# Hybrid recurrent decoder step: modulated blocks kept in two parts, S5 columns in another layout

## The chip, the cores and the metric

One core of one Trainium2 chip runs the whole step in one launch. The metric is the device time of the program in microseconds.

## What is computed

One layer on a prompt of 2048 tokens and 8 samples of 4 tokens (2080 columns), width 1024, float32 in and out. The part that the change touches:

```
mod = silu(c) @ ada_w + ada_b                     # six sections of 1024: sh1 sc1 g1 sh2 sc2 g2
h   = x * (1 + sc1) + sh1                         # modulated input
z   = h @ in_proj                                 # 1024 x 1536
gate_a, xa, xb = z[:, :512], z[:, 512:1024], z[:, 1024:]
hseq = rglru(conv4(xa, state_conv), state_h)      # RG-LRU group
y_s  = s5(xb)                                     # 32 groups of 16 columns, each a 64-wide complex diagonal state
gy   = gelu(y_s); y_b = gy * sigmoid(gy @ glu_w + glu_b)
mix  = concat(gelu(gate_a) * hseq, y_b) @ out_proj
x = layer_norm(alpha * x + g1 * mix);  then a squared-ReLU MLP with sh2, sc2, g2 and a second layer norm
```

## The kernel before

TensorE multiplies in a 4-byte format in which each operand is split into a high and a low part: a product is three matmuls (high x high, high x low, low x high). `split` makes the two parts: ScalarE copies the value into the high part, then a given engine (VectorE `V` or GpSimd `Q`) subtracts it to get the low part. The framework plans the order of the instructions of each engine ahead of time from its own estimates; an engine then works through its order and waits where data is missing. Nearly all DMAs are issued by SyncE (`SP`), in order, on one queue.

The tokens are cut into 8 blocks of 256 (block 7 has the 32 sample columns too). Two passes go over them.

First pass (to about 165 us). `make_h` loads a block of x, transposes it on TensorE, applies scale and shift into the float32 tile `hf` (two halves q of 4 x 128 features; two buffers in all), stores `hf` to the DRAM tensor `Hd` (L434), and splits it into `hh` and `hl` (the low part of half 1 on GpSimd, of half 0 on VectorE). `proj` (L373 to L375) multiplies the block by the four S5 column tiles of `in_proj`; ScalarE copies the result into `xb`, ordered by position j in a chunk of 8 tokens and chunk c, and `put_u` (L512) stores it to `Ud[m, j, p, c]`, in pieces of 32 chunks, 128 bytes. Blocks 0 and 1 (`BARE` = 2) are treated before the shift sh1 is known and get it later. Between the blocks the S5 matrices are prepared (tiles `Bx`, `CA`, `kt`).

Second pass (about 165 to 465 us). `load_w` loads and splits the eight gate and RG-LRU column tiles of `in_proj` (raw tile `rwin`, parts `hwin` and `lwin`; the low part alternates between GpSimd and VectorE). `load_h` (L553) loads a block of `Hd` again, float32, and splits it again with the low part on GpSimd (`b0l` to `b7l` in the rows). For each of 8 blocks and 8 column tiles `proj` gives one result (`accg`, 24 matmuls), stored to `Xd` or `Gd`. Sixteen S5 pairs are interleaved, one every 2.25 column tiles: `load_pair` loads `U` from `Ud` (L1743, two loads of 128 rows of 1088 bytes), matrices `M` and `Tf`, builds the rotations `E` by doubling (VectorE with ScalarE), and splits; `scan_pair` multiplies (`pv`), copies 8 columns to `VS`, scans along the chunks and splits the states (`Hh`, `Hl`); `out_pair` makes `py`. Also interleaved are the four other sections of the adaLN product: `ada_mm` adds up (`pa`), and `ada_fin` copies the sum to SBUF (`adasb`, VectorE, L190), transposes it with four small matmuls (`pm`, L193) and adds the bias. From block 5 on the RG-LRU group starts: `rg_weights` loads the conv and recurrent states `sct` and `sht` and transposes them (`pst`), `rg_conv` makes `xc` on VectorE.

Then come the GLU and output projection with the first norm (about 465 to 750 us) and the MLP; the change does not touch them.

Of the kernel before, what the change touches and what calls it, by code (L numbers as in the profile page):

```python
# [35 lines left out]
def trunk(ctx: ExitStack, tc: tile.TileContext, *args):  # L36
# [53 lines left out]
    Hd = dtile([KD, P, T], "Hd")  # L90
    Ud = dtile([4, L, P, NC2], "Ud")
# [96 lines left out]
    def ada_fin(pa, sec):  # L188
        sb = raw_tile(f"adasb{sec}")[:, 0:512]
        V.tensor_copy(sb, pa)  # L190
        pm = ptile([P, 4, 2, 9], "C", f"pm{sec}")
        for k in range(4):
            PE.matmul(pm[:, k, :], sb[:, k * P:k * P + P], sel, start=True, stop=True)  # L193
        add(V, mods[:, sec * 8:sec * 8 + 8, :].rearrange("p (n k) s -> p k n s", n=2), pm,
            vec["ada_b"][:, sec * 8:sec * 8 + 8].rearrange("p (n k) -> p k n", n=2).unsqueeze(3).to_broadcast([P, 4, 2, 9]))
# [49 lines left out]
    def rg_weights(rg):  # L245

        wgh = rg.tile([P, 2, 4, P], F32R, tag="wgh", name="wgh")
        wgl = rg.tile([P, 2, 4, P], F32R, tag="wgl", name="wgl")
        wgr = rg.tile([P, 2, 4, P], F32, tag="xc", name="wgr", bufs=2)
        Q.memset(wgr, 0.0)  # L250
        for g, key in enumerate(("rg_wr", "rg_wi")):
            src = a[key][0].rearrange("(f q) i j -> q i f j", q=2)
            for q in range(2):
                SP.dma_start(wgr[64 * q:64 * q + 64, g, :, 64 * q:64 * q + 64], src[q])
        split(wgh, wgl, wgr, Q)

        sct = rg.tile([24, 512], F32, tag="rr", name="sct")
        SP.dma_start(sct, a["state_conv"][0].rearrange("s w f -> (s w) f"))
        sht = rg.tile([8, 512], F32, tag="gi", name="sht")
        SP.dma_start(sht, a["state_rglru_h"][0])  # L260
        pst = gate_ps[0]("pst")[:, 0:128].rearrange("p (f c) -> p f c", f=4)
        for f in range(4):
            PE.transpose(pst[:, f, 0:24], sct[:, f * P:f * P + P], ident[:24, :24])
            PE.transpose(pst[:, f, 24:32], sht[:, f * P:f * P + P], ident[:8, :8])
        xas = rg.tile([P, 4, NS, 7], F32, tag="xas", name="xas")
        V.tensor_copy(xas[:, :, :, 0:3], pst[:, :, 0:24].rearrange("p f (s w) -> p f s w", w=3))
        h0s = rg.tile([P, 4, NS], F32, tag="h0s", name="h0s")
        V.tensor_copy(h0s, pst[:, :, 24:32])
        rgs.update(wgh=wgh, wgl=wgl, xas=xas, h0s=h0s, h=None)
# [92 lines left out]
    with lpool("ab") as ab:  # L362
# [31 lines left out]
        def make_h(hb):  # L394
# [10 lines left out]
            for q in range(2):  # L405
# [28 lines left out]
                SP.dma_start(Hd[4 * q:4 * q + 4, :, t0:t0 + nt].rearrange("k p t -> p k t"), hf[:, :, :nt])  # L434
                hh, hl = hs[q]
                if hb:
                    split(hh[:, :, :nt], hl[:, :, :nt], hf[:, :, :nt], Q if q else V)
                if hb == BARE:
                    split(hh[:, :, 256:258], hl[:, :, 256:258], SH1[:, 4 * q:4 * q + 4, 0:1].to_broadcast([P, 4, 2]), V)
# [68 lines left out]
        def put_u(hb, m, xb, shift=None):  # L508
            ncc = 32 + (16 if hb == 7 else 0)
            if shift is not None:  # L510
                ts(V, xb[:, :, 0:32], xb[:, :, 0:32], shift, None, ALU.add)
            u_out[hb] = SP.dma_start(Ud[m, :, :, hb * 32:hb * 32 + ncc].rearrange("j p c -> p j c"), xb[:, :, :ncc]).ins  # L512

        for hb in range(8):
# [8 lines left out]
            for m in range(4):  # L523
# [6 lines left out]
                else:  # L530
                    xb = ab.tile([P, L, 48], F32, tag="stg", name=f"xb{hb}_{m}", bufs=4)
                act(xb[:, :, 0:32], acc[:, 0:256].rearrange("p (c j) -> p j c", j=L), AF.Copy)
                if hb == 7:
                    Q.memset(xb[:, :, 40:48], 0.0)
                    Q.memset(xb[:, 0:4, 32:40], 0.0)
                    act(xb[:, 4:8, 32:40], acc[:, 256:288].rearrange("p (s j) -> p j s", j=JS), AF.Copy)
# [9 lines left out]
        def load_h(hb):  # L546
            t0, nt = piece(hb)
            hs = halves(f"b{hb}")
            for q in range(2):
                hh, hl = hs[q]  # L550
                hf = ab.tile([P, 4, 288], F32, tag="hf", name=f"hg{hb}_{q}", bufs=2)
                dst = hf[:, :, :nt]
                SP.dma_start(dst, Hd[4 * q:4 * q + 4, :, t0:t0 + nt].rearrange("k p t -> p k t"))  # L553
                if hb < BARE:
                    for kk in range(4):
                        k = 4 * q + kk
                        if kk % 2:
                            ts(V, dst[:, kk, :], dst[:, kk, :], SH1[:, k, 0:1], None, ALU.add)
                        else:
                            act(dst[:, kk, :], dst[:, kk, :], AF.Identity, bias=SH1[:, k, 0:1])  # L560
# [3 lines left out]
        wga = [load_w(m, V if m % 2 else Q, wpa if m in (4, 5, 6, 7, 0) else wpb, u_out[WB])  # L564
               for m in (4, 5, 6, 7, 0, 1, 2, 3)]
        nxt = load_h(0)
        npair = nada = 0
        spare = [f32(wslot(f"spare{i}", "l", wpb)).rearrange("p (q h c) -> p q h c", q=2, h=2) for i in range(2)]
        RG_AT = 5
        PAIR_U = [2.25 * i for i in range(17)] + [99]  # L570
        for hb in range(8):
            t0, nt = piece(hb)
            hs = nxt
            if hb < 7:
                nxt = load_h(hb + 1)
            if hb == RG_AT:
# [12 lines left out]
            for m in range(8):  # L589
# [5 lines left out]
                st = ab.tile([P, 384], F32, tag="stg", name=f"st{hb}_{m}", bufs=4)  # L595
# [3 lines left out]
                if nada < 32 and 2 * (u + 1) // 3 > nada + 1:  # L599
# [6 lines left out]
                    if k == KD - 2:  # L606
                        ada_fin(pa, sec)
# [849 lines left out]
def s5(ctx, nc, tc, a, outs, rpool, ps, ident, scratch, o):  # L1457
# [278 lines left out]
    def load_pair(p):  # L1736
# [3 lines left out]
        U = pt_([P, 2, NC2], f"U{p}", "U", bufs=2)  # L1740
        for h in range(2):
            r0 = (g0 + h) * 16
            SP.dma_start(U[:, h, :], Ud[b, :, r0:r0 + 16, :])  # L1743
# [19 lines left out]
        split(Uh, Ul, U, Q)  # L1763
# [135 lines left out]
```

## Time and profile before

| | |
|---|---|
| median of 3 runs | 2112.32 us (2111.28 to 2117.05) |
| profiled execution | 2115.44 us, its span 2113.7 us |
| granted TensorE clock, mean | 0.986 |
| TensorE busy | 2011.9 us, 95% |
| VectorE busy | 1543.5 us, 73% |
| ScalarE busy | 1087.4 us, 51% |
| GpSimd busy | 494.0 us, 23% |
| DMA queue of SyncE | 359415 packets, 485.52 MB, 69.6% of 16 engines |

A matmul's shown duration overlaps the next one, so busy TensorE is not TensorE at its peak; its waits and the spacing of its matmuls tell more. Shares over the whole span mix stages with different limits, so the stretches of the first 480 us are read one by one.

### The profile page before, as it was taken

The page shows a single profiled execution, that of the slowest core. Times are in us where ns is not written, and L with a number is a line of the kernel's source. Part 1 is how long each engine was busy: PE and PEld are TensorE (multiplying, and loading weights), DVE is VectorE, ACT ScalarE, POOL GpSimd, SP SyncE. Part 2 cuts the span into 40 slices and gives each one's busy share as a digit, 9 for nine tenths or more (in the row PEclk, how much of TensorE's full clock was granted, in tenths as well). Part 3 has the DMA queues.
Part 4 walks back from the last instruction along what each step waited for, and adds up shares of the span by engine and source line. Part 5 has one row for each costly group of instructions (what it writes and reads, how often), then busy time and mean ns, then how long its engine had stood idle before and what let it go on. Part 6 is the DMA issues. An engine that isn't in the chain of part 4 may idle for free.

```text
span 2113.7 us, 35579 instructions
## 1 busy us (share of the span) xinstructions
PE 2011.9 (95%) x13055; PEld 1904.1 (90%) x13055; DVE 1543.5 (73%) x2920; ACT 1087.4 (51%) x2077; POOL 494.0 (23%) x327
## 2 busy tenths in 40 slices
PE   7998999889999989999999899999999999999996
PEld 4897888887877879999999899999999999999996
DVE  5678897467887899989898965666747555655587
ACT  3446665445766447554646454635445344444452
POOL 2255333323433233222223300101012001010103
PEclk9999999999999999999999999999999999999998
DMA  9799765543434467968677797878678968686861
GB/s 329 177 263 274 233 197 171 141 137 80 130 94 99 134 244 265 346 248 306 239 278 264 266 323 248 305 268 288 243 260 317 315 229 282 216 270 239 265 218 54
DMA packets 363037, 489.08 MB, mean 231 GB/s; under 512 B 126939, under 2 KB 264575, under 8 KB 362863
## 3 DMA queue, kind: packets, MB, share of 16 engines
q1 hardware_dynamic: 359415, 485.52, 69.6%
q8 instruction: 103, 1.69, 0.3%
q10 hardware_dynamic: 3448, 1.29, 0.2%
q14 instruction: 71, 0.58, 0.1%
HBM read 347.73 MB, written 139.00 MB: 230 GB/s over the span
## 4 chain that ended last, share of the span: by engine, by line
PE 63%; DVE 19%; DMA 6%; issue 5%; ACT 4%; POOL 1%; SPq 1%; ACTq 0%; DVEq 0%; POOLq 0%
PE m1a L1078 19%; PE m2x L1225 13%; PE m1s L1078 8%; PE m2s L1225 6%; PE m2a L1225 3%; DVE xc L62 2%; DVE acc L44 1%; PE accg L373 1%; PE accg L374 1%; PE accg L375 1%; PE op L963 1%; PE pa L185 1%; PE op L964 1%; PE op L962 1%; DVE gi L347 1%
## 5 line engine op out<-in xcount | busy, mean ns | idle before, releaser
L44 POOL TENSOR_TENSOR y<-y,ln_g 128x512 f32<-128x512 f32 (+3 forms) x28 | 36.5, 1320 | 645.8 <-ACT y L65 544.2
L65 ACT ACTIVATE hid<-hid 128x346 f32<-128x346 f32 (+1 forms) x240 | 116.1, 489 | 71.1 <-DVE hid L62 64.3
L65 ACT ACTIVATE ht<-hid 128x692 fp32r<-128x692 f32 (+1 forms) x92 | 72.0, 783 | 127.8 <-PE m2a L1225 38.9
L44 DVE TENSOR_TENSOR lt<-hid,ht 128x692 fp32r<-128x692 f32 (+1 forms) x92 | 85.2, 927 | 40.5 <-ACT ht L65 40.5
L44 DVE TENSOR_TENSOR acc<-m2x,acc 128x346 f32<-128x346 f32 (+1 forms) x168 | 84.1, 511 | 32.0 <-PE m2x L1225 31.7
L44 DVE TENSOR_TENSOR hid<-hid,hid 128x692 f32<-128x692 f32 (+1 forms) x92 | 87.1, 947 | 23.5 <-ACT hid L65 23.3
L1225 PE MATMUL m2x<-ht,hw2s 128*128 128x348 f32 (+1 forms) x352 | 87.7, 322 | 1.8 <-DVE acc L44 1.8
L62 DVE SCALAR_TENSOR_TENSOR hid<-m1s,vecB,u 128x346 f32<-128x346 f32 (+1 forms) x94 | 53.5, 573 | 45.0 <-ACT u L65 35.4
L65 ACT ACTIVATE u<-m1a 128x346 f32<-128x346 f32 (+1 forms) x96 | 43.5, 453 | 70.4 <-PE m1a L1078 63.0
L44 DVE TENSOR_TENSOR lb<-hid,hb 128x692 fp32r<-128x692 f32 (+1 forms) x69 | 69.2, 1004 | 4.7 <-ACT hb L65 4.5
L65 ACT ACTIVATE hb<-hid 128x692 fp32r<-128x692 f32 (+1 forms) x69 | 53.8, 783 | 21.6 <-PE m2a L1225 6.9
L1225 PEld LDWEIGHTS m2x<-ht,hw2s 128*128 128x128 f32 x352 | 61.9, 189 | 2.2 <-ACT hw2s L65 2.1
L65 ACT ACT_TABLE_LOAD x40 | 51.3, 1283 | 15.9 <-DVE hgb L57 6.5
L44 DVE TENSOR_TENSOR acc<-m2s,acc 128x346 f32<-128x346 f32 (+1 forms) x120 | 55.7, 508 | 4.1 <-PE m2s L1225 4.0
L1078 PE MATMUL m1s<-h2t13h,hw1s 128*128 128x348 f32 (+1 forms) x200 | 54.1, 329 | 3.9 <-DVE x L62 3.5
L1225 PE MATMUL m2x<-lt,hw2s 128*128 128x348 f32 (+1 forms) x176 | 56.1, 321 | 0.9 <-DVE lt L44 0.9
L1225 PE MATMUL m2x<-ht,w2s 128*128 128x346 f32 (+1 forms) x216 | 55.9, 321 | 0.0
L1225 PE MATMUL m2s<-ht,hw2s 128*128 128x348 f32 (+1 forms) x208 | 53.2, 331 | 2.6 <-ACT ht L65 2.6
L44 DVE TENSOR_TENSOR u<-m1s,u 128x346 f32<-128x346 f32 (+1 forms) x48 | 24.7, 514 | 42.0 <-PE m1s L1078 27.2
L65 ACT ACTIVATE y<-y,AB,mods 128x128 f32<-128x128 f32 (+2 forms) x96 | 37.5, 472 | 34.5 <-DMA y<-Cd 34.5
L1225 PE MATMUL m2a<-hb,hw2a 128*128 128x348 f32 (+1 forms) x200 | 52.0, 327 | 3.4 <-DVE acc L44 3.4
L1078 PE MATMUL m1a<-h2b1h,hw1a 128*128 128x348 f32 (+1 forms) x208 | 55.1, 323 | 0.0
(854 smaller groups left out, 7982.0 us busy)
## 6 DMA issues: line engine op xcount, KB each, us to landing
W1d<-hw1s SPq DMA_DIRECT2D x53, 512.0 KB
W2d<-hw2s SPq DMA_DIRECT2D x53, 512.0 KB
w1s<-W1d SPq DMA_DIRECT2D x45, 512.0 KB
lw1s<-W1d SPq DMA_DIRECT2D x43, 512.0 KB
hw2s<-W2d SPq DMA_DIRECT2D x41, 512.0 KB
hw1s<-W1d SPq DMA_DIRECT2D x40, 512.0 KB
w2s<-W2d SPq DMA_DIRECT2D x40, 512.0 KB
lw2s<-W2d SPq DMA_DIRECT2D x39, 512.0 KB
```

The lines of the kernel that those rows point to most:

```text
L44: return eng.tensor_tensor(out=out, in0=in0, in1=in1, op=op)
L62: return V.scalar_tensor_tensor(out, in0, s, in1, op0, op1)
L65: return S.activation(out, in_, f, **kw).ins
L185: PE.matmul(pa[q:q + 32, :], cT[:, k + e, :], w[:, n * 512:n * 512 + 512], start=(k == 0), stop=(k == KD - 2), tile_position=(0, q))
L347: V.tensor_tensor_scan(gi[:, f, :n], rr[:, f, :n], gi[:, f, :n], 0.0 if pi == 0 else rgs["h"][:, f:f + 1], ALU.mult, ALU.add)
L373: PE.matmul(acc[:, :nt], wh[:, k, :], hh[:, kk, :nt], start=(k == 0), stop=False)
L374: PE.matmul(acc[:, :nt], wh[:, k, :], hl[:, kk, :nt], start=False, stop=False)
L375: PE.matmul(acc[:, :nt], wl[:, k, :], hh[:, kk, :nt], start=False, stop=(k == KD - 1))
L962: PE.matmul(ac[:w, :], yh[:, kk, o:o + w], wh[:, hs], start=(k == 0), stop=False)
L963: PE.matmul(ac[:w, :], yl[:, kk, o:o + w], wh[:, hs], start=False, stop=False)
L1078: PE.matmul(ps, x[:, k, :], h[:, k, o:o + w], start=(on is None and k + i == 0), stop=(k == 3 and i == 2), skip_group_check=on is not None)
L1225: PE.matmul(ps[2 * s_ + jj], x[:, f, js], h[:, f, :], start=(fresh and n + f + e == 0), stop=(n == len(pairs) - 1 and f + e == 3), skip_gr ...
```

## The change

Five edits. Blocks 2 to 7 of the modulated input are no longer stored as float32 `Hd` but as their two parts in a new tensor `Hsd`, after the split; the second pass loads the parts straight into `hh` and `hl` and splits nothing for these blocks. `Ud` gets the layout [tile, column, block, position, chunk], so that a block's columns are stored as rows of 1 KB (2 KB for block 7, whose sample columns become a ninth block), and the load of a pair gathers its [position x column] rows from pieces of 32 chunks. The low parts of all gate weights are made on VectorE. `ada_fin` is cut in two: the copy to SBUF comes where it was, the small matmuls three column tiles later. The conv and recurrent states are loaded at block 4 into the `hf` buffers, not inside `rg_weights`.

```diff
-    Hd = dtile([KD, P, T], "Hd")
-    Ud = dtile([4, L, P, NC2], "Ud")
+    Hd = dtile([KD, P, 512], "Hd")
+    Hsd = dtile([2, KD, P, T], "Hsd")
+
+    Ud = dtile([4, P, 9, L, 32], "Ud")
...
-    def ada_fin(pa, sec):
+    def ada_out(pa, sec):
         sb = raw_tile(f"adasb{sec}")[:, 0:512]
         V.tensor_copy(sb, pa)
+        return sb
+
+    def ada_fin(pa, sec, sb=None):
+        if sb is None:
+            sb = ada_out(pa, sec)
...
-        sct = rg.tile([24, 512], F32, tag="rr", name="sct")
-        SP.dma_start(sct, a["state_conv"][0].rearrange("s w f -> (s w) f"))
-        sht = rg.tile([8, 512], F32, tag="gi", name="sht")
-        SP.dma_start(sht, a["state_rglru_h"][0])
+        sct, sht = rgs["in"]
...
-                SP.dma_start(Hd[4 * q:4 * q + 4, :, t0:t0 + nt].rearrange("k p t -> p k t"), hf[:, :, :nt])
+                if hb < BARE:
+                    SP.dma_start(Hd[4 * q:4 * q + 4, :, t0:t0 + nt].rearrange("k p t -> p k t"), hf[:, :, :nt])
                 hh, hl = hs[q]
                 if hb:
                     split(hh[:, :, :nt], hl[:, :, :nt], hf[:, :, :nt], Q if q else V)
+                if hb >= BARE:
+                    for i, x in enumerate((hh, hl)):
+                        SP.dma_start(Hsd[i, 4 * q:4 * q + 4, :, t0:t0 + nt].rearrange("k p t -> p k t"), f32(x[:, :, :nt]))
...
-            u_out[hb] = SP.dma_start(Ud[m, :, :, hb * 32:hb * 32 + ncc].rearrange("j p c -> p j c"), xb[:, :, :ncc]).ins
+            n = 2 if hb == 7 else 1
+            u_out[hb] = SP.dma_start(Ud[m, :, hb:hb + n].rearrange("p b j c -> p (b j c)"), xb.rearrange("p j c -> p (j c)")).ins
...
                 hh, hl = hs[q]
+                if hb >= BARE:
+                    for i, x in enumerate((hh, hl)):
+                        SP.dma_start(f32(x[:, :, :nt]), Hsd[i, 4 * q:4 * q + 4, :, t0:t0 + nt].rearrange("k p t -> p k t"))
+                    continue
...
-        wga = [load_w(m, V if m % 2 else Q, wpa if m in (4, 5, 6, 7, 0) else wpb, u_out[WB])
+        wga = [load_w(m, V, wpa if m in (4, 5, 6, 7, 0) else wpb, u_out[WB])
...
+            if hb == RG_AT - 1:
+                rgs["in"] = [ab.tile([P, 4, 288], F32, tag="hf", name=f"rgin{i}", bufs=2).rearrange("p f t -> p (f t)")
+                             [:n, 0:512] for i, n in enumerate((24, 8))]
+                SP.dma_start(rgs["in"][0], a["state_conv"][0].rearrange("s w f -> (s w) f"))
+                SP.dma_start(rgs["in"][1], a["state_rglru_h"][0])
...
                     if k == KD - 2:
-                        ada_fin(pa, sec)
+                        fins.append((u + 3, pa, sec, ada_out(pa, sec)))
+                while fins and u >= fins[0][0]:
+                    ada_fin(*fins.pop(0)[1:])
...
-        U = pt_([P, 2, NC2], f"U{p}", "U", bufs=2)
+        U = pt_([P, 2, 288], f"U{p}", "U", bufs=2)
         for h in range(2):
             r0 = (g0 + h) * 16
-            SP.dma_start(U[:, h, :], Ud[b, :, r0:r0 + 16, :])
+            SP.dma_start(U[:, h, :].rearrange("p (b c) -> p b c", c=32), Ud[b, r0:r0 + 16].rearrange("k b j c -> j k b c"))
...
-        split(Uh, Ul, U, Q)
+        split(Uh, Ul, U[:, :, 0:NC2], Q)
```

## Rows read from the trace of the kernel before

**Rows 1.** Stretches: limits, length, busy us and instructions, clock, DMA share, GB/s.

```profile
75.00:165.00 90.00, 85.70 (x737) 82.85 (x737) 68.27 (x99) 43.93 (x90) 40.27 (x29) 0.98 0.99 253
165.00:205.00 40.00, 36.17 (x279) 32.49 (x278) 35.93 (x53) 24.43 (x51) 24.51 (x14) 0.96 0.94 262
205.00:400.00 195.00, 186.05 (x1464) 158.02 (x1462) 156.09 (x357) 114.43 (x311) 61.80 (x57) 1.00 0.67 200
409.00:419.00 10.00, 9.60 (x80) 9.39 (x80) 0.46 (x1) 8.08 (x15) 6.99 (x3) 1.00 0.40 138
```

(The five busy columns are PE, PEld, DVE, ACT and POOL.)

**Rows 2.** TensorE in order of time: start, us, work, idle before and its releaser.

```profile
161.72 0.40 PE L373 MATMUL accb<-a7h,hwin 128*128 128x288 f32 x1 [1.63 <-ACT xb L65]
184.31 0.60 PE L1780 MATMUL pv<-Uh,Mh 128*128 128x272 f32 x1 [3.12 <-DVE VS L1785]
250.80 0.39 PE L1780 MATMUL pv<-Uh,Mh 128*128 128x272 f32 x1 [0.89 <-ACT Mh L65]
290.26 0.39 PE L1827 MATMUL py<-Hh,Mh 64*128 64x272 f32 x2 [2.24 <-ACT Hh L65]
334.35 0.39 PE L1827 MATMUL py<-Hh,Mh 64*128 64x272 f32 x2 [1.46 <-ACT Hh L65]
378.10 0.21 PE L263 MATMUL pst<-ident,sct 24*128 24x24 f32 x1 [1.00 <-DMA sct<-in_state_conv_dram]
403.84 1.47 PE L193 MATMUL pm<-sel,adasb 128*128 128x18 f32 x6 [4.97 <-DVE adasb L190]
```

**Rows 3.** Stretches as in rows 1, at the lower clock.

```profile
183.70:187.20 3.50, 2.89 (x13) 2.89 (x14) 1.89 (x6) 2.30 (x5) 0.00 (x0) 0.51 0.96 323
402.20:409.10 6.90, 5.26 (x25) 5.26 (x25) 2.30 (x8) 1.34 (x3) 0.00 (x0) 0.51 0.78 145
```

**Rows 4.** VectorE in order of time around 400 us.

```profile
383.71 4.95 DVE L62 SCALAR_TENSOR_TENSOR xc<-xa,vecB,xc 128x256 f32<-128x256 f32 x12
...
396.00 7.19 DVE L62 SCALAR_TENSOR_TENSOR xc<-xa,vecB,xc 128x256 f32<-128x256 f32 x12
403.11 0.68 DVE L190 COPY adasb<-pa 128x512 f32<-128x512 f32 x1
```

**Rows 5.** In order of time: a split's copy and subtraction, and VectorE's scans.

```profile
192.15 1.26 DVE L1795 TENSOR_TENSOR_SCAN V<-rho,V 128x256 f32<-128x256 f32 x2
194.73 1.06 ACT L65 ACTIVATE b2h<-hg 128x1024 fp32r<-128x1024 f32 x1 [0.99 <-PE accg L375]
...
280.13 3.40 DVE L1795 TENSOR_TENSOR_SCAN V<-rho,V 128x256 f32<-128x256 f32 x2
280.19 5.51 POOL L44 TENSOR_TENSOR b4l<-hg,b4h 128x1024 fp32r<-128x1024 f32 x2 [3.21 <-ACT b4h L65]
```

**Rows 6.** DMA packets of 92 to 95.5, 398.9 to 400, 404.9 to 406.2 us.

```profile
DMA packets 4022, 0.51 MB, mean 145 GB/s; under 512 B 4022, under 2 KB 4022, under 8 KB 4022
...
DMA packets 1027, 0.13 MB, mean 118 GB/s; under 512 B 1027, under 2 KB 1027, under 8 KB 1027
q1 hardware_dynamic: 1027, 0.13, 75.0%
...
DMA packets 409, 0.42 MB, mean 322 GB/s; under 512 B 0, under 2 KB 409, under 8 KB 409
```

(The first are stores of S5 columns, the second one load of `Yd` in 128-byte pieces, the third a load in 1-KB rows.)

**Rows 7.** Issues of the pair's load and of the block's store: shortest, median, longest ns.

```profile
L1743 SPq DMA_DIRECT2D U<-Ud x32: 577/617/1910, 163.1 to 323.2; - x32
L434 SPq DMA_DIRECT2D Hd<-hf x16: 359/686/2795, 20.0 to 147.9; - x16
```

**Rows 8.** In order of time at the seam: GpSimd and VectorE.

```profile
176.80 2.38 POOL L44 TENSOR_TENSOR lwin<-rwin,hwin 128x1024 fp32r<-128x1024 f32 x1
181.09 2.34 POOL L44 TENSOR_TENSOR b1l<-hg,b1h 128x1024 fp32r<-128x1024 f32 x1 [1.90 <-ACT b1h L65]
...
181.38 2.46 DVE L62 SCALAR_TENSOR_TENSOR E<-E,et 128x128 f32<-128x128 f32 x2 [0.79 <-ACT et L65]
185.94 1.23 DVE L44 TENSOR_TENSOR lwin<-rwin,hwin 128x1024 fp32r<-128x1024 f32 x1 [1.61 <-ACT hwin L65]
```

More of the change, by code (lines that the diff above doesn't have):

```diff
@@ L508, in put_u @@
         def put_u(hb, m, xb, shift=None):
-            ncc = 32 + (16 if hb == 7 else 0)
             if shift is not None:
-                ts(V, xb[:, :, 0:32], xb[:, :, 0:32], shift, None, ALU.add)
-            u_out[hb] = SP.dma_start(Ud[m, :, :, hb * 32:hb * 32 + ncc].rearrange("j p c -> p j c"), xb[:, :, :ncc]).ins
+                ts(V, xb, xb, shift, None, ALU.add)
+            n = 2 if hb == 7 else 1
+            u_out[hb] = SP.dma_start(Ud[m, :, hb:hb + n].rearrange("p b j c -> p (b j c)"), xb.rearrange("p j c -> p (j c)")).ins
         for hb in range(8):
@@ L530, in trunk @@
                 else:
-                    xb = ab.tile([P, L, 48], F32, tag="stg", name=f"xb{hb}_{m}", bufs=4)
-                act(xb[:, :, 0:32], acc[:, 0:256].rearrange("p (c j) -> p j c", j=L), AF.Copy)
+                    xb = ab.tile([P, 16, 32], F32, tag="stg", name=f"xb{hb}_{m}", bufs=4)[:, 0:16 if hb == 7 else L]
+                act(xb[:, 0:L], acc[:, 0:256].rearrange("p (c j) -> p j c", j=L), AF.Copy)
                 if hb == 7:
-                    Q.memset(xb[:, :, 40:48], 0.0)
-                    Q.memset(xb[:, 0:4, 32:40], 0.0)
-                    act(xb[:, 4:8, 32:40], acc[:, 256:288].rearrange("p (s j) -> p j s", j=JS), AF.Copy)
+                    Q.memset(xb[:, L:16], 0.0)
+                    act(xb[:, 12:16, 0:8], acc[:, 256:288].rearrange("p (s j) -> p j s", j=JS), AF.Copy)
                 if hb >= BARE:
@@ L553, in load_h @@
                 SP.dma_start(dst, Hd[4 * q:4 * q + 4, :, t0:t0 + nt].rearrange("k p t -> p k t"))
[L554 to L560, printed above, removed]
+                for kk in range(4):
+                    k = 4 * q + kk
+                    if kk % 2:
+                        ts(V, dst[:, kk, :], dst[:, kk, :], SH1[:, k, 0:1], None, ALU.add)
+                    else:
+                        act(dst[:, kk, :], dst[:, kk, :], AF.Identity, bias=SH1[:, k, 0:1])
                 split(hh[:, :, :nt], hl[:, :, :nt], dst, Q)
             return hs
-        wga = [load_w(m, V if m % 2 else Q, wpa if m in (4, 5, 6, 7, 0) else wpb, u_out[WB])
+        wga = [load_w(m, V, wpa if m in (4, 5, 6, 7, 0) else wpb, u_out[WB])
                for m in (4, 5, 6, 7, 0, 1, 2, 3)]
@@ L567, in trunk @@
         npair = nada = 0
+        fins = []
         spare = [f32(wslot(f"spare{i}", "l", wpb)).rearrange("p (q h c) -> p q h c", q=2, h=2) for i in range(2)]
@@ L594, in trunk @@
                 acc = proj(wga[m], hs, nt, f"accg{hb}_{m}")
-                st = ab.tile([P, 384], F32, tag="stg", name=f"st{hb}_{m}", bufs=4)
+                st = ab.tile([P, 512], F32, tag="stg", name=f"st{hb}_{m}", bufs=4)
                 act(st[:, :nt], acc[:, :nt], AF.Copy if m < 4 or hb in RAW_GATE else AF.Gelu_apprx_tanh)
```

## The prediction

> **What bounds the kernel now.** I read the table of stretches first, to see which engine is close to its limit where, then TensorE's waits in order of time in the two projection passes, then what the engine that ended each wait had been doing, and last the DMA packets around. Everything that the change touches lies before 480 us; behind that the code is the same, so whatever is won or lost before 480 us is taken to reach the end unchanged.
>
> In the table of stretches [rows 1] TensorE is busy 85.7 of 90 us in the first pass (75 to 165 us), 36.2 of 40 at the seam between the passes and 186 of 195 in the second pass. Undisturbed it issues 80 matmuls in 10 us, 0.12 us each. So TensorE bounds these passes, and only its waits can be won. VectorE is nearly full as well (35.9 of 40 at the seam, 156 of 195 in the second pass), and the DMA engines are full until 205 us (0.99, 0.94) and at 0.67 after.
>
> The waits are few [rows 2]; in brackets stands what ended each. 1.63 us at 161.72 (a staged S5 column tile not yet free); 3.12 us at 184.31 (VectorE's copy of VS); 0.89, 2.24 and 1.46 us at 250.80, 290.26 and 334.35 (pairs, behind ScalarE copies that follow VectorE); 1.00 us at 378.10 (the load of the conv state); 4.97 us at 403.84 (VectorE's copy of the last adaLN sum). [...] TensorE works again from 184.31 and 403.84, so it loses half of 2.9 and of 5.3 us: 1.45 and 2.6 us.
>
> **Part 1, the adaLN sum finished later.** At 403.11 VectorE gets to the copy that section 5's sum waits for, after twelve convolution steps that took 7.19 us; twelve like them took 4.95 us before [rows 4]. The change issues the copy as before and its TensorE half three column blocks later. A block is 24 matmuls, 2.9 us, so 8.6 us of other matmuls stand between, more than the wait of 4.97. They need only their blocks, loaded long before. What is late next is nothing that I see: the same VectorE steps also lose the GpSimd work of part 2. Gain 4.97 + 2.6 = 7.6 us. If the planner leaves the sum where it is, the wait shrinks only by the 2.2 us that the steps were held up.
>
> **Part 2, the blocks stored as two parts.** For blocks 2 to 7 the second pass loses its split: twelve ScalarE copies of about 1.06 us and twelve GpSimd subtractions of about 2.4 us (two of them, 5.51 us, at 280.19) [rows 5]. TensorE waits for none of them. They count through VectorE: two scans that take 1.26 us at 192.15 take 3.40 us at 280.13, exactly while GpSimd subtracts block 4's lower part [rows 5], and the pair behind them is the wait of 2.24 us at 290.26. The waits at 250.80 and 334.35 follow blocks 3 and 5 in the same way. These three are 4.6 us; I take 4.0, since GpSimd keeps the pairs' own subtractions, which VectorE meets too.
>
> It costs DMA. Each block moves 1.05 MB more out and 1.05 MB more in (block 7 1.18). Rows of 1 KB move at 322 GB/s [rows 6], 3.1 us for 1 MB. Blocks 3 to 7, 5.4 MB, go out in the first pass from 75 us on: +16.7 us; block 2 goes out in the idle time before. In, block 2 costs 3.3 us at the seam and blocks 3 to 7 16.7 us later. On SP's queue it is twelve more issues out and twelve more in, at about 0.6 us as other issues there [rows 7]. A store now waits for GpSimd's or VectorE's lower part instead of the sum alone, and S5 column stores and x loads queue behind it. In return the hf buffers wait for no store any more, so block 0 of the second pass can be loaded earlier.
>
> **Part 3, the S5 columns.** Stores of 128-byte pieces run at 145 GB/s: 4022 pieces in 3.5 us, 0.87 us for a store of 1024 [rows 6]. In rows of 1 KB it is 0.41 us, so 29 stores of the first pass give back 13 us. The pair's load now takes 1152 pieces of 128 bytes. The nearest row is the load of Yd, 1024 such pieces in 75% of 1.1 us, 0.83 us [rows 6], so 0.93 us against 0.43 us for 139 KB in long rows: +0.5 us for each of 32 loads. Its issue on SP takes 0.62 us now [rows 7]; a source of four indices has no row, and I keep 0.6 to 1.2 us.
>
> Added up, the DMA engines have 89 + 16.7 - 13 = 93 us of work in the 90 us of the first pass; at the seam 37.6 + 3.3 + 8 x 0.5 = 45 in 40; after it 131 + 16.7 + 12 = 160 in 195. They come up to 8 us late by 205 us and catch up afterwards. x and adaLN loads are issued 10 us or more ahead, gate weights are not. The cost lies between 0 and 8 us; I take 2. The wait at 161.72 could go (faster column stores) or grow (two parts of block 7 ahead of them); I take 0.
>
> [...]
>
> **Part 4, the gate weights' lower parts on VectorE.** Four subtractions leave GpSimd (2.38 us each) and cost VectorE 1.23 us each [rows 8], 4.9 us in a stretch where it is 90% busy. Against that, two rotation steps on VectorE take 2.46 us at 181.38 while GpSimd works on block 1 from 181.09 [rows 8]; work of that kind is what stands ahead of the VS copy that TensorE waits for at 184.31. Block 1 is still split on GpSimd, only earlier. The wait with its clock loss is 3.12 + 1.45 = 4.6 us; I take half, 2.3. The added VectorE work costs 0 to 2 us of it where GpSimd would not have blocked it; I take 0.5.
>
> **Part 5, the states loaded a block earlier.** The wait of 1.00 us at 378.10 goes. Two loads leave SP's queue in front of the convolution; they are hidden under block 4.
>
> **Sum.** -7.6 - 4.0 - 2.3 - 1.0 + 2 + 0.5 = -12.4 us. The profiled execution took 2115.44 us, which gives 2103; the median of the runs shown is 2112.32, and against it the forecast is **2100 us**.
>
> **Rivals.** (a) All named waits close and DMA costs nothing: 7.6 + 4.6 + 4.6 + 1.0 + 1.6 = 19.4 us, 2093, and some us less if freed VectorE also shortens waits too small to stand in the rows. For it: VectorE is nearly full. Against: the DMA sums. (b) DMA takes it back: the full 8 us late on TensorE's path, the 184.31 wait stays, and the edits give 7.6 + 1.0 + 4.0 - 8 - 2 = 2.6 us: 2110; or the sum of part 1 stays where it was: 2107. (c) Slower: the turning load. After 205 us the DMA engines have 195 - 131 - 16.7 = 47 us free for 24 loads, so the load may cost up to 0.43 + 2 = 2.4 us before the engines, and TensorE waiting for U, are the bound of the second pass. At 3.3 us per load it is 24 x 0.9 = 22 us over: 2100 + 22 = 2122. For it: no row shows this pattern, and SP's in-order queue would feel a split into several issues as well. Against: the Yd load at 0.83 us. [...]
>
> **How the numbers follow.** Forecast 0.50 (2093 to 2106); (a) 0.14 (2086 to 2093); (b) 0.21 (2106 to 2118); (c) 0.13; (d) 0.02. About 0.3%, 6.3 us, is what a measurement of this kernel can tell from no change: faster is under 2106. So faster 0.64, same 0.21, slower 0.15. The range goes from 2088, half of (a), to 2117, nearly all of (b); what is left out is 0.07 below and 0.16 above.
>
> **What would show it.** Right: no TensorE wait for adasb near 400 us and no low clock there; no scan at twice its length in the second pass; DMA share under 0.9 after 205 us; a U load that takes about 1 us. Wrong: TensorE waits that a DMA ends (U, rwin, ada) between 150 and 210 us, S5 column tiles not free, VectorE waiting at the seam, or another order of the planner with new waits that no row of before shows.

## The result, and the profile after

| | before | after |
|---|---|---|
| median | 2113.15 us (6 runs, 2109.27 to 2117.05) | 2136.03 us (6 runs, 2129.22 to 2143.06) |
| ratio after / before | | 1.0112, 95% interval 1.0087 to 1.0136 |
| profiled execution, its span | 2115.44, 2113.7 us | 2129.22, 2127.4 us |
| first pass ends | 164.9 us | 161.8 us |
| second pass ends | 463.6 us | 479.4 us |
| second pass to the end | 1650.1 us | 1648.0 us |

The change makes the kernel 1.1% slower. The ends of the passes are the starts of the last matmuls on `accb` and `accg`. The profiled execution after is the fastest of its six, so that the passes add up to 13.7 us of the 22.9 us between the medians. The first pass gained 3.1 us; the second takes 317.6 us for 298.7; behind it nothing moved. Block 4 of the second pass begins at 348.6 us for 322.4, so from 3 us ahead the kernel fell 26 behind, 29 us lost while the S5 pairs run. Blocks 6 and 7, where the adaLN wait was, won 8 back (68.9 us before, 394.7 to 463.6; 61.0 after, 418.4 to 479.4).

The table of stretches of the kernel after (limits, length, busy us of PE, PEld, DVE, ACT, POOL, clock, DMA share, GB/s), to be held against [rows 1]:

```profile
75.00:165.00 90.00, 88.13 (x762) 86.00 (x760) 66.66 (x95) 44.10 (x88) 34.80 (x23) 0.98 0.99 329
165.00:205.00 40.00, 36.39 (x275) 33.39 (x273) 30.94 (x65) 24.37 (x58) 11.93 (x10) 0.91 0.76 195
205.00:400.00 195.00, 170.69 (x1270) 141.93 (x1269) 131.27 (x326) 92.83 (x279) 28.15 (x43) 0.96 0.79 218
400.00:480.00 80.00, 74.86 (x595) 71.87 (x594) 44.09 (x75) 42.99 (x74) 28.50 (x13) 1.00 0.55 158
```

From 205 to 400 us TensorE is busy 171 us for 186 before, at a clock of 0.96 for 1.00. VectorE is no longer full (131 for 156 us); as the kernel is 26 us behind there, this alone does not show that part 2 freed it. On the mean the DMA engines are not full (0.79). What TensorE waited for from 205 to 350 us, after and then before (line, releaser: us in total, times, longest):

```profile
PE py L1838 <- ACT Th L65: 9.6, 4, 4.7
PE pa L187 <- DMA ada<-in_ada_w_dram: 6.4, 2, 5.4
PE pv L1798 <- ACT Mh L65: 4.6, 4, 1.9
PE pa L187 <- DMA hada<-in_ada_w_dram: 2.2, 2, 2.0
```

```profile
PE py L1827 <- ACT Hh L65: 3.7, 2, 2.2
PE pv L1780 <- ACT Mh L65: 1.4, 2, 0.9
PE pv L1782 <- DVE Ml L44: 1.0, 3, 0.6
PE py L1827 <- DVE Hl L44: 0.4, 1, 0.4
```

After, these are 22.8 us of waits for data that a load brings (`Th` and `Mh` are the copies of the loaded `Tf` and `M`); before, the list has 6.5 us, of which 2.4 for the parts of `M` and none for `Th` or a load. The waits for the scanned states (`Hh`, `Hl`), 4.1 us before, are gone. One of the waits for `Th`, followed back in order of time on SP's queue, ScalarE and TensorE, with the stretch behind it:

```profile
267.72 1.28 SPq L1851 DMA_DIRECT2D Yd<-Yt  x2
...
269.64 0.38 SPq L1764 DMA_DIRECT2D M<-BCd  x1
...
273.82 0.61 SPq L1761 DMA_DIRECT2D U<-Ud  x1
274.53 4.98 SPq L1851 DMA_DIRECT2D Yd<-Yt  x2
279.56 0.60 SPq L1761 DMA_DIRECT2D U<-Ud  x1
280.26 2.43 SPq L1764 DMA_DIRECT2D M<-BCd  x1
282.74 1.28 SPq L1766 DMA_DIRECT2D M<-BCd  x2
284.12 1.01 SPq L614 DMA_DIRECT2D Xd<-st  x2
285.22 0.40 SPq L1770 DMA_DIRECT2D Tf<-Td  x1
288.29 0.42 ACT L65 ACTIVATE Th<-Tf 128x256 fp32r<-128x256 f32 x1 [5.04 <-DMA Tf<-Td]
288.76 0.59 PE L1838 MATMUL py<-Uh,Th 128*128 128x272 f32 x1 [4.71 <-ACT Th L65]
287.00:290.00 3.00, 1.24 (x5) 1.24 (x6) 1.05 (x4) 1.67 (x6) 0.00 (x0) 0.50 0.92 243
```

The column behind the start is how long SP was at an issue. The two stores of `Yd` behind the turned `U` load hold SP for 4.98 us, the `M` load behind the second one for 2.43; the same issues took 1.28 and 0.38 us at 267.72 and 269.64, so these two alone put `Tf` 5.8 us late. ScalarE waits 5.04 us for it, TensorE 4.71, and the clock falls to 0.50. And while SP is held, the packets of three stretches:

```profile
DMA packets 301, 0.95 MB, mean 318 GB/s; under 512 B 48, under 2 KB 75, under 8 KB 301
q1 hardware_dynamic: 301, 0.95, 97.1%
DMA packets 627, 0.18 MB, mean 178 GB/s; under 512 B 606, under 2 KB 606, under 8 KB 625
q1 hardware_dynamic: 625, 0.15, 67.8%
DMA packets 510, 0.08 MB, mean 77 GB/s; under 512 B 504, under 2 KB 509, under 8 KB 509
q1 hardware_dynamic: 509, 0.07, 47.0%
```

These are 274.5 to 277.5, 277.5 to 278.5 and 278.5 to 279.5 us. In the first 3 us the engines are busy (97%) with 0.95 MB, for the most part the 4-KB rows of the two adaLN loads that SP issued at 272.83 and 273.32, ahead of the `U` load. Only then come 1110 pieces under 512 bytes, nearly all of the 1152 of the load issued at 273.82. They take some 2.0 us, with the engines at 68% and 47%; SP is let go as they end, at 279.5. So the pieces of the turned load stand about 3 us behind that traffic and then take 2 us to move, and SP waits for both.

### The profile page after: what moved, and what is told of

It is laid out like the page before. It is cut to its first block, busy times and chain, and to the rows that moved or that the text cites. A ratio compares the mean times of both kernels' runs of the same rounds, so it can differ in the third digit from the quotient of the medians.

```text
span 2127.4 us, 35544 instructions
## 1 busy us (share of the span) xinstructions
PE 2019.1 (95%) x13055; PEld 1910.7 (90%) x13055; DVE 1526.2 (72%) x2924; ACT 1076.6 (51%) x2065; POOL 456.0 (21%) x307
## 4 chain that ended last, share of the span: by engine, by line
PE 63%; DVE 19%; DMA 7%; issue 4%; ACT 4%; SPq 2%; POOL 1%; ACTq 0%; DVEq 0%; POOLq 0%
PE m1a L1096 19%; PE m2x L1243 13%; PE m1s L1096 8%; PE m2s L1243 6%; PE m2a L1243 3%; DVE xc L62 1%; DVE acc L44 1%; PE pa L187 1%; PE accb L378 1%; PE accb L377 1%; PE accb L379 1%; PE accg L377 1%; PE accg L378 1%; PE accg L379 1%; DVE gi L351 1%
## 5 line engine op out<-in xcount | busy, mean ns | idle before, releaser
L980 PE MATMUL op<-hwo,ybh 128*128 128x512 f32 x128 | 51.6, 406 | 2.8 <-ACT ybh L65 2.8
L65 ACT ACTIVATE hid<-m1a,vecB 128x346 f32<-128x346 f32 (+1 forms) x48 | 26.2, 547 | 53.7 <-PE m1a L1096 53.6
```

Of the source, the lines that this page charges most:

```text
L65: return S.activation(out, in_, f, **kw).ins
L980: PE.matmul(ac[:w, :], yh[:, kk, o:o + w], wh[:, hs], start=(k == 0), stop=False)
```

## The experiments

The theory, called T1 in the expectations, was that the pair's turned load is the loss, by holding SP's in-order queue; the rivals (T2, T3) were the doubled transfers of the two-part blocks, the gate parts on VectorE, and another order of the planner, which plans all engines anew whenever a transfer's shape changes. In the table, passes and end are those of the profiled execution in us, the ratio is that to the kernel before in runs on the same chip.

| kernel | median | ratio (95%) | first pass ends | second pass takes | second pass to end |
|---|---|---|---|---|---|
| without part 3 | 2119.11 | 1.0032 (1.0019 to 1.0044) | 174.0 | 291.4 | 1656.1 |
| without part 2 | 2136.20 | 1.0120 (1.0090 to 1.0149) | 171.3 | 306.8 | 1653.5 |
| part 3 alone | 2143.04 | 1.0139 (1.0113 to 1.0165) | 173.6 | 307.8 | 1665.3 |
| long rows, planned anew | 2105.68 | 0.9968 (0.9947 to 0.9990) | 161.7 | 279.3 | 1657.6 |
| long rows, order of after | 2102.97 | 0.9953 (0.9938 to 0.9968) | 164.1 | 285.2 | 1653.4 |
| turned, order of long rows | 2139.09 | 1.0124 (1.0105 to 1.0142) | 161.7 | 315.2 | 1659.6 |
| 512 pieces | 2114.59 | 1.0001 (0.9991 to 1.0012) | 161.1 | 295.3 | 1657.4 |
| 1152 pieces, other walk | 2115.97 | 1.0022 (1.0011 to 1.0032) | 161.6 | 297.3 | 1655.2 |
| U on ScalarE's queue | 2138.43 | 1.0121 (1.0098 to 1.0145) | 161.8 | 313.8 | 1662.7 |
| Tf on ScalarE's queue | 2127.35 | 1.0065 (1.0049 to 1.0082) | 161.1 | 310.1 | 1654.7 |
| part 1 alone | 2114.49 | 1.0005 (0.9996 to 1.0014) | 163.9 | 294.7 | 1651.4 |
| part 2 alone | 2118.92 | 1.0025 (1.0016 to 1.0034) | no comparable trace | | |
| parts 1, 4, 5 | 2114.70 | 1.0005 (0.9996 to 1.0014) | 165.2 | 299.2 | 1647.1 |
| part 1, split off ScalarE | 2126.58 | 1.0065 (1.0050 to 1.0080) | 163.8 | 295.7 | 1665.2 |
| paired stores | 2101.65 | 0.9948 (0.9931 to 0.9965) | 159.2 | 283.8 | 1655.4 |
| paired stores, no part 2 | 2119.68 | 1.0032 (1.0020 to 1.0043) | 166.6 | 295.8 | 1655.7 |

### Which part

**Without part 3.** Layout, store and load of `Ud` as before, the rest as after.

```diff
-    Ud = dtile([4, P, 9, L, 32], "Ud")
+    Ud = dtile([4, L, P, NC2], "Ud")
...
+            SP.dma_start(U[:, h, :], Ud[b, :, r0:r0 + 16, :])
```

> The changed kernel with part 3 alone undone (S5 columns stored and loaded as before; the other four parts stay). Theory T1, that the pair's turning load (1152 pieces of 128 bytes) is the loss, by holding SP's in-order queue: the 25 to 28 us lost between 194 and 349 us go, the adaLN sum's 7.9 us stay won, some us of the first pass may be given back since column stores of 1024 pieces return; 2098 to 2107 us, ratio 0.993 to 0.998 to the kernel before. Rival T2, that the doubled transfers of the two-part blocks are the loss: the second pass stays long, 2125 us or more. Rival T3, that VectorE's added gate parts or another order of the planner is the loss: 2125 us or more too.

The loss in the second pass went (291.4 us, 7.3 less than before), so there is none without part 3. But it was slower than the theory's 2098 to 2107: the first pass ends 9.1 us late. Its DMA share from 75 to 165 us is 1.01, and TensorE does 674 matmuls there for 762 in the kernel after:

```profile
75.00:165.00 90.00, 80.17 (x674) 76.94 (x672) 55.74 (x87) 36.99 (x67) 30.31 (x14) 0.97 1.01 273
```

**Without part 2.** `Hd` for all blocks and the split on load again.

```diff
-                if hb >= BARE:
-                    for i, x in enumerate((hh, hl)):
-                        SP.dma_start(Hsd[i, 4 * q:4 * q + 4, :, t0:t0 + nt].rearrange("k p t -> p k t"), f32(x[:, :, :nt]))
```

> The changed kernel with part 2 alone undone (blocks stored once as before and split again on load). T1 (the turning load): still slower than before, 2125 to 2140 us, and SP's issues of U loads still up to 4 us and more. T2 (the two-part blocks): 2100 to 2110 us.

In time as the theory said: without the two-part blocks the kernel is as slow. But its second pass takes 306.8 us for the 317.6 of the kernel after, 8.1 above the kernel before; the other 10 us of its loss (profiled executions) lie in the first pass (171.3 for 164.9) and behind the second. So the turned load costs without part 2 too, and more beside it, as far as two programs that were planned apart can show.

**Part 3 alone**, in the kernel before (the diff of the change's `Ud`, `xb`, `put_u` and `U` lines).

> The kernel before with part 3 alone. T1: it carries the whole loss without the 8 us of the adaLN sum, 2128 to 2142 us, with TensorE waits between 205 and 350 us that ScalarE's Th or the adaLN loads end. T2 and T3: 2100 to 2113 us, since the column stores of the first pass get faster.

In time slightly above the theory's range, but not by its account alone. Of the 33 us in the profiled executions 9.1 lie in the second pass (307.8 us), 8.7 in the first (173.6 for 164.9) and 15.2 behind the second. Here, and in the run without part 2, the first pass itself ends 6 to 9 us late, at a DMA share of 0.77 to 0.80, with TensorE waiting 4.3 and 5.5 us for `xb` copies from 110 to 180 us. These programs were planned anew throughout; which reordering does it was not settled. That the time met the theory is in part luck.

### The load, or the plan

**Long rows.** The 147 KB of a load in 128 rows of 1152 bytes; the S5 input then lies in another order, so the output is not the layer's, but the amount of work is the same (this holds for the next runs with exchanged patterns too).

```diff
-            SP.dma_start(U[:, h, :].rearrange("p (b c) -> p b c", c=32), Ud[b, r0:r0 + 16].rearrange("k b j c -> j k b c"))
+            SP.dma_start(U[:, h, :], Ud[b, r0:r0 + 16].rearrange("k b j c -> k (b j c)").rearrange("k (j x) -> j k x", j=L))
```

> The changed kernel, but each pair's load reads the same 147 KB in rows of 1152 bytes, so 128 pieces for 1152; the S5 input is then in the wrong order, the work is the same. T1: as with the old layout or a little better, 2095 to 2107 us, U issues on SP back at about 0.6 us. If something else in the new layout (the larger U tile, the padded last block, the stores) costs the time: 2125 us or more.

At the upper end of what was expected, 30 us below the kernel after. But the planner's order is another one too, which the next two runs take apart: the planned program is kept, with every order and wait, and only the access patterns of the 32 loads are exchanged behind the planner.

```diff
         trunk(tc, *args)
+    reread(nc, False)
...
+                    sa, da = [[288, 8], [2304, 16], [1, 288]], [[576, 128], [1, 1], [1, 288]]
+                rows[i] = x.__replace__(ins=[s.__replace__(ap=sa, bass_ap=None)], outs=[d.__replace__(ap=da, bass_ap=None)])
```

> The planned program of the changed kernel, instruction for instruction in its order and with its waits, but with the 32 U loads re-pointed after planning to rows of 1152 bytes (the S5 input is then in the wrong order). The earlier run with long rows was also planned anew, so its 30 us could be the load itself or the other order. If the load itself is the cost: about as that run, 2100 to 2110 us. If the plan made for the turned load is the cost: 2125 us or more. Half and half lies between.

The other way round the long rows are planned and the turned pattern `[[32, 8], [256, 144], [1, 32]]` is put in:

> The reverse: the order planned for the long rows, with the U loads turned after planning (the output is that of the changed kernel). If the load itself is the cost: 2125 to 2140 us, with SP's issues of U loads up to 4 us and more again. If the plan is the cost: about 2106 us.

The load itself it is: 33 us in one order (2136.03 to 2102.97), 33 us in the other (2139.09 to 2105.68); the order counts for 3. Issue and waits of the same program with long rows, from 205 to 350 us (the `U` issue's shortest, median and longest in ns, then TensorE's waits), and the `U` issue of the kernel after:

```profile
L1780 SPq DMA_DIRECT2D U<-Ud x32: 594/620/1871, 168.4 to 315.9; - x32
PE pv L1817 <- ACT Mh L84: 1.0, 2, 0.6
PE pa L206 <- DMA ada<-in_ada_w_dram: 0.3, 1, 0.3
```

```profile
L1761 SPq DMA_DIRECT2D U<-Ud x32: 597/616/5837, 165.2 to 346.9; - x32
```

The median issue is the same; the longest is 5.84 us for 1.87. TensorE's waits fall from 22.8 to 1.3 us. With the clock of 0.96 for 1.00 over 195 us, at most 7.8 us, this is up to 29 of the 32.4 us between the two second passes.

A long-row load is not done much sooner. One is issued at 266.38 us, and its pieces move until about 269.7; in the last of these microseconds little else moves, 101 pieces at a DMA share of 0.32. But SP is not held behind it:

```profile
266.38 0.62 SPq L1780 DMA_DIRECT2D U<-Ud  x1
268.89 1.31 SPq L1870 DMA_DIRECT2D Yd<-Yt  x2
DMA packets 101, 0.11 MB, mean 112 GB/s; under 512 B 9, under 2 KB 99, under 8 KB 101
q1 hardware_dynamic: 101, 0.11, 31.8%
```

The two `Yd` stores behind it are issued in 1.31 us, the first of them while it moves (the packets are 268.5 to 269.5 us). So by these two stretches (4.98 us behind 1152 pieces, 1.31 us behind 128) what holds SP is the number of pieces in the queue, more than the time of the transfer; the next section varies that number.

### What makes the load slow

**512 pieces** of 288 bytes, same plan, same bytes (`sa, da = [[72, 8], [576, 64], [1, 72]], [[576, 128], [72, 4], [1, 72]]`).

> The planned program of the changed kernel with the U loads re-pointed to the same bytes in 512 pieces of 288 bytes instead of 1152 of 128 (the S5 input is then in the wrong order). 128 pieces gave 2103 us, 1152 gave 2136. If the cost goes by the number of pieces: 33 x 384 / 1024 = 12 us above 2103, 2112 to 2118 us. If there is a threshold that 512 pieces stay under: 2103 to 2107 us.

12 us above long rows (10 by the ratios), as the count of pieces says; 512 pieces are not free.

**1152 pieces, other walk:** same pieces and addresses, but `[[256, 144], [32, 8], [1, 32]]`, so that the 144 pairs of column and block are the outermost index and the 8 positions the inner one.

> The planned program of the changed kernel, its U loads still 1152 pieces of 128 bytes from the same addresses, but walked with the 144 (column, block) pairs outermost and the 8 positions inside (the S5 input is then in the wrong order). If half of the DMA engines is what makes the load slow: a load's pieces arrive in about 1.0 us instead of 2.0, the DMA share in such a stretch is 0.9 and not 0.5, and the kernel takes 2105 to 2118 us. If the number of pieces alone counts, whatever the engines: 2130 us or more.

The same pieces cost 13 us above long rows (15 by the ratios) instead of 33. From 211 to 212 us, and from 308 to 309, where such loads run, and last a microsecond of the kernel after, 227.5 to 228.5, in which only a turned load moves:

```profile
DMA packets 1478, 0.24 MB, mean 239 GB/s; under 512 B 1427, under 2 KB 1477, under 8 KB 1477
q1 hardware_dynamic: 1477, 0.23, 131.1%
...
DMA packets 1662, 0.22 MB, mean 216 GB/s; under 512 B 1655, under 2 KB 1662, under 8 KB 1662
q1 hardware_dynamic: 1662, 0.22, 135.9%
...
DMA packets 793, 0.10 MB, mean 101 GB/s; under 512 B 793, under 2 KB 793, under 8 KB 793
q1 hardware_dynamic: 793, 0.10, 64.3%
```

In that microsecond the turned load moves 793 pieces at a share of 0.64, the other walk up to 1655 at 1.36. Worked out from these shares of 16 engines, a piece takes the same engine time in both, 13 ns, so no single piece is slower in the turned load; half as many are under way at once (the pieces and the shares both differ by a factor of 2.1). Why they are half was not shown: whether the turned load goes over half of the engines, as the expectation supposes, can't be read here, since the trace has the engines' share together and not by number.

So the number of pieces alone is not the price (the other walk has as many and costs 13 us for 33), and the outermost index alone is not either: the long rows have 8 there like the turned load, and the kernel is 33 us faster with them.

### The queue

**U on ScalarE's queue.**

```diff
-            SP.dma_start(U[:, h, :].rearrange("p (b c) -> p b c", c=32), Ud[b, r0:r0 + 16].rearrange("k b j c -> j k b c"))
+            S.dma_start(U[:, h, :].rearrange("p (b c) -> p b c", c=32), Ud[b, r0:r0 + 16].rearrange("k b j c -> j k b c"))
```

> The changed kernel with the U loads issued on ScalarE's queue, still turned. If the turned load costs by holding SP's queue: SP's other issues are short again (below 1 us for Tf and M) and the waits for Tf go, while ScalarE is held instead at its own issues; ScalarE is busy half of the time there, so 2105 to 2125 us. If the DMA engines are too slow with 128-byte pieces: Tf, M and U stay late, 2130 us or more.

Half right: SP is free, `Tf` issues take 0.58 us at most. But the hold moved with the load, and nothing was won. The issue rows and TensorE's longest wait from 165 to 350 us:

```profile
L1761 ACTq DMA_DIRECT2D U<-Ud x32: 589/1144/7447, 162.6 to 344.1; - x32
L1770 SPq DMA_DIRECT2D Tf<-Td x16: 359/384/576, 169.1 to 358.4; - x16
PE accg L377 <- ACT st L65: 18.4, 5, 7.6
```

ScalarE is held up to 7.4 us in an issue, and the copies out of PSUM stand behind it.

**Tf on ScalarE's queue**, `U` on SP:

```diff
-        SP.dma_start(Tf, bass.AP(tensor=td.tensor, offset=td.offset, ap=[[512, P], [16 * 512, 8], [1, 32]]))
+        S.dma_start(Tf, bass.AP(tensor=td.tensor, offset=td.offset, ap=[[512, P], [16 * 512, 8], [1, 32]]))
```

> The changed kernel with only the 16 loads of Tf, the largest wait behind SP's queue (35.7 us of ScalarE's waits), issued on ScalarE's queue. If SP's queue is what makes them late: the wait of Th for Tf goes and with it the TensorE waits for Th (10.5 us), 2115 to 2127 us. If the DMA engines make them late: no change, 2130 us or more.

9 us better than the kernel after, just outside what a held SP queue was to give: ScalarE's waits for `Tf` fall from 35.7 to 9.3 us (165 to 500 us), and TensorE's waits for `Th` go. Waiting behind SP is a real part of the price. The other 24 us of the 33 are not recovered by this; `M` and the adaLN weights still stand behind SP, and TensorE waits 2.7 and 4.3 us for them from 205 to 350 us.

### The other parts

**Part 1 alone** (`ada_out`, `fins`), in the kernel before.

> The kernel before with part 1 alone (the adaLN sum's small matmuls three column tiles later). By the prediction -7.6 us, 2105 us, with no TensorE wait for the copy adasb and no low clock near 405 us. If the wait only moves: 2110 us or more.

No gain, though the second pass ends 5.0 us earlier: what follows, up to the last GLU matmul, takes it back (463.6 to 703.6 us before, 458.6 to 703.4 here). Blocks 6 and 7 gain 8 us as in the kernel after (397.8 to 458.6); the blocks ahead of them, planned anew, lose 4. **Parts 1, 4 and 5:**

> The kernel before with parts 1, 4 and 5 and neither of the two layout edits. By the prediction's terms -7.6 - 2.3 + 0.5 - 1.0 = -10.4 us: 2102 us. If the two-part blocks of part 2 are needed for that (VectorE freed of GpSimd's subtractions): 2105 us or more. A rival, that other plans move the later stages by as much: anywhere from 2098 to 2112.

No gain either, and here not even at the end of the second pass. In order of time:

```profile
412.00 1.06 ACT L65 ACTIVATE hgy<-gy 128x1024 fp32r<-128x1024 f32 x1 [7.88 <-DMA gy<-Yd]
412.97 0.37 ACT L65 ACTIVATE st<-accg 128x256 f32<-128x256 f32 x1
413.39 0.58 PE L375 MATMUL accg<-b6h,hwin 128*128 128x256 f32 x1 [4.59 <-ACT st L65]
```

The wait for the adaLN copy, 4.97 us [rows 2], is gone; in its place ScalarE waits 7.88 us for the load of `gy` (the first GLU block), and the copy `st` that frees TensorE's bank stands behind it: 4.59 us.

**Part 1 with that split taken off ScalarE:**

```diff
+            Q.tensor_copy(gyh[:, :, :n], gy[:, :, :n])
+            sub(Q, gyl[:, :, :n], gy[:, :, :n], f32(gyh[:, :, :n]))
```

> Part 1 alone, with the first GLU block's split taken off ScalarE (both steps on GpSimd), so that ScalarE's copies out of PSUM no longer stand behind the load of gy. If that wait is where part 1's 7.6 us went: the second pass ends 6 to 10 us before that of the kernel before, and 2104 to 2109 us. If the next stage takes it back in any case: 2112 us or more, with the second pass still early.

Wrong: the second pass ends where part 1 alone ended, and the stages behind lose 14 us (1665.2 for 1651.4), TensorE waiting 11.7 us for VectorE in the GLU (5.8 in part 1 alone). The run tested little: in part 1 alone ScalarE waits only 1.90 us for `gy`, the 7.88 us belong to parts 1, 4 and 5 together. Whether the split on GpSimd or the new plan costs the 14 us was not settled.

**Part 2 alone:**

> The kernel before with part 2 alone (blocks 2 to 7 stored as two parts, S5 columns still stored in 1024 pieces). The DMA engines then have 89 + 16.7 = 106 us of work in the 90 us of the first pass: if that counts, the first pass ends 8 to 12 us late, and against the 4 us that VectorE gains the kernel is slower, 2116 to 2122 us. If the transfers are hidden: 2108 us.

Slower by 5 us, as full DMA engines in the first pass would have it; that the first pass is the place was not shown in this run.

### A version that beats both

**Paired stores.** Old layout and long-row load; the columns of two blocks wait in one tile and are stored in 256-byte pieces. The other four parts stay; the loads of x and of the gate weights are let go by the stores of other blocks, since there are fewer stores.

```diff
-                    xb = ab.tile([P, L, 48], F32, tag="stg", name=f"xb{hb}_{m}", bufs=4)
+                    if hb % 2 == 0:
+                        xpair[m] = ab.tile([P, L, 80 if hb == 6 else 64], F32, tag="stg2", name=f"xb{hb}_{m}", bufs=6)
+                    xb = xpair[m]
+                at = 32 * (hb % 2) if hb >= BARE else 0
...
-                if hb >= BARE:
+                if hb >= BARE and hb % 2:
                     put_u(hb, m, xb)
```

> Parts 1, 2, 4 and 5 with the old layout of the S5 columns, loaded in long rows, but the columns of blocks 2 and 3, 4 and 5, 6 and 7 stored together, in pieces of 256 bytes instead of 128: half the pieces. With single stores this was 2119 us, its first pass ending 9 us late. If the store pieces were that loss: the first pass ends at 161 to 166 us and the kernel takes 2103 to 2110 us, below both kernels. If the two-part stores were it: 2115 us or more.

2101.65 us, 0.5% below the kernel before and 1.6% below the kernel after. **The same without part 2:**

> The same paired stores with parts 1, 4 and 5, without the two-part blocks. Single stores gave 2114.7 us. The first pass has DMA time to spare here without them, so its end moves by 3 us at most: 2108 to 2115 us. If this is as fast as the run with part 2, part 2 is worth nothing by itself.

Slower than expected and than the kernel before. Between the two, part 2 is worth 18 us, 12 of them in the second pass (295.8 to 283.8) and 7 in the first (166.6 to 159.2); as the two were planned apart, how much of this is the plan is open. VectorE's 32 scans, with part 2 and without, as groups (busy us, mean ns):

```profile
L1820 DVE TENSOR_TENSOR_SCAN V<-rho,V 128x256 f32<-128x256 f32 x32 | 20.8, 674 | 0.0
```

```profile
L1811 DVE TENSOR_TENSOR_SCAN V<-rho,V 128x256 f32<-128x256 f32 x32 | 27.1, 876 | 0.0
```

The median scan takes 678 ns in both. Four of the 32 take 1.8 to 2.8 us without part 2, none more than 0.69 us with it. TensorE's waits for the scanned states (`Hh`, `Hl`) in the second pass fall with them from 7.5 to 0.4 us.

Not tried: `U` on GpSimd's queue.

## Why the prediction was wrong, step by step

The forecast was 2100 us and the range ended at 2117; it came to 2136.

**The views** were right about what bounds the kernel: TensorE's waits, and VectorE behind them.

**The step that failed** is the price of the turned load in part 3. The prediction took it from the load of `Yd`, 0.83 us for 1024 pieces [rows 6], and wrote 0.93 us, +0.5 for each of 32. Measured: 2.0 us where one was followed, and 33 us in the kernel for 32 loads, by exchanging the pattern alone. The row has the same piece size but not the same walk, and with the other walk twice the pieces move in a us. The prediction's unit made it worse: it counted engine time, and by engine time the load was priced about right (1.15 us at most, 67.8% and 47.0% of a us each). What it left out is that the pieces hold the queue: "I keep 0.6 to 1.2" for the issue was right at the median (0.62 us) and wrong where it counted, up to 5.84 us, and the issues behind were held as well (4.98 us at 274.53). Rows 7 could have warned: the longest `U` issue there is 1.91 us, and that of the block's store 2.80 us, at a median of 0.62 and 0.69.

**The DMA sums** (93 of 90, 45 of 40, 160 of 195 us; 2 us taken) were the wrong frame in the second pass: the share was 0.79, as 160 of 195 says (0.82), and 29 us were lost all the same. For the first pass they are not settled: with the edits of both layouts the pass ends 3.1 us earlier, with part 2 and single stores 9.1 us late, at a share of 1.01. That would make the 13 us that the long-row stores give back worth about 12 us on the path; but these programs were planned apart, and two others end the pass 6 and 9 us late at a share of 0.77 to 0.80. (A store of 1024 pieces is 0.89 us by the row, not 0.87; nothing hangs on it.)

**Rival (c)** named the load, the side and, from the sums, a point from which it decides (2.4 us) that was near the 2.0 measured. Its mechanism was wrong: the engines did not become the bound of the pass (0.79), SP's queue did, which it mentions only for a load split into several issues.

**Part 1, -7.6 us:** inside the change it came true: there is no wait for `adasb`, the clock stays 1.00 from 395 to 412 us, blocks 6 and 7 gain 8 us. (Its 2.6 us of clock loss, and the 1.45 of part 4, come from [rows 3]: 5.3 us of work from 403.84 to 409.10 and 2.9 from 184.31 to 187.20, at a granted clock of 0.51.) Alone it gave 0, though blocks 6 and 7 gain as much. "What is late next is nothing that I see" is the step that failed here: with part 1 alone the blocks ahead and the GLU stage took it back, and together with parts 4 and 5 the load of `gy` in front of ScalarE's copies.

**Part 2, -4.0 us for VectorE:** the mechanism is borne out where it was read: in the kernel after no scan takes over 0.69 us, and TensorE's waits for `Hh` and `Hl` (4.1 us before, from 205 to 350 us) are gone. That the waits at 250.80 and 334.35 follow blocks 3 and 5 "in the same way" is not: of the 32 scans of the kernel before only one is long (2.80 us, the one at 280.13). The worth of the part depends on what stands beside it: 12 us gained in the second pass with paired stores, but 10.8 lost with the turned load (306.8 us without part 2, 317.6 with it).

**Parts 4 and 5, -2.3 + 0.5 - 1.0 us:** the waits for `VS` at 184 us and for `sct` at 378 us are gone in the kernel after. At the seam others took their place (2.26 us for `Mh` at 183.35, 1.18 for `st` at 185.05), and the clock there is 0.91 for 0.96. Together with part 1 they gave 0; no gain of theirs was shown.

**The sum:** with the load's price taken out, the changed kernel is 9.8 us faster than before (2102.97 to 2112.81) and the forecast, which had 2 us for all of the DMA, was 12.4. That is no confirmation: the terms behind it were wrong on both sides (parts 1, 4 and 5 -10.4 forecast, 0 measured alone; parts 2 and 3 without the load -2 forecast, the rest of 9.8 measured).

**The premise** that what is won before 480 us reaches the end holds for the kernel after (1648.0 for 1650.1 us) and not in general: over the kernels here this part, unchanged in the code (but for one split in one run) and planned anew, takes 1647.1 to 1665.3 us in single executions, a spread of more than most edits are worth.

**The 0.43 us for long rows** is no measurement: the prediction worked it out from the 322 GB/s of [rows 6], and where a long-row load could be followed it moved for more than 1 us. The turned load took 2.0 us, 4.7 times the 0.43. A load dearer than the 3.3 us of rival (c), to which (d) gives 0.02, is shown by no run: the 32 turned loads cost the kernel 33 us together, about 1 us each.

## What to carry to other kernels

Price a DMA by the pieces that it puts into the issuing engine's queue and by who stands behind them there, not only by its bytes or its share of 16 engines: here issues behind a load of 1152 pieces were held for up to 5 us, the last 2 of them with the engines half idle (shares of 0.68 and 0.47). Before an access pattern is turned, look at its outermost index (8 and 144 differed by a factor of two in pieces moved in a us, 793 and up to 1655), and look at the longest issues of the rows, not at the median. When one wait on an in-order engine is removed, read off what that engine's next instruction waits for; and if small pieces are needed on one side, put them where the queue has nothing urgent and make them longer (two blocks together) instead of moving them to the side that other loads wait behind.

## What the runs showed of the hardware that was not expected

Pieces of this load that waited in the queue held the engine that issued, at the load's own issue or at the one behind it: SP up to 5.84 us and ScalarE up to 7.45 us at an issue of the load (0.62 us at the median on SP), SP 4.98 us at the two stores behind it. A load of the same bytes in 128 pieces did not, in the stretch that was followed (1.31 us for the two stores behind it, at 268.89 us). Pieces of 128 bytes moved at 793 in a us with 8 as outermost index (227.5 to 228.5 us) and at 1427 to 1655 with 144. The share that the DMA view shows passes 100% (131.1%, 135.9%) with such pieces, so 0.64 there was half of what it can show, and 1.0 need not be full.
